# Stationary-weight products of a two-layer decoder: both parts of the activation in one 512-column pass, halves added by VectorE

## The chip, the cores and the metric

The kernel runs on one core of one Trainium2 chip. The metric is the device time of one execution in microseconds (us). The core has a matrix engine (TensorE, PE in the rows, with its weight loads as PEld), a vector engine (VectorE, DVE), a scalar engine (ScalarE, ACT), GpSimd (POOL) and a DMA queue driven by SyncE (SP). Matrix products are accumulated in PSUM banks of 128 x 512 fp32 values and taken out of them by ACT or DVE.

## The reference

Two decoder layers on x of 256 tokens by 1024 channels, in fp32. Each layer:

```python
proj = x @ w_in                       # q, k, v, u_ssm (512), u_pool (512), 3 x 1024 gate logits
attn_out = sliding_window_attention(q, k, v, sinks) @ w_br_attn
ssm_out  = glu_after_gelu(s5_ssm(u_ssm, ...), w_glu) @ w_br_ssm
pool_out = multiscale_pool(u_pool, pool_w, pool_scale) @ w_br_pool
gates = sigmoid(gate_logits + b_gate)            # one 1024-wide gate per branch
h = (gates[0]*attn_out + gates[1]*ssm_out + gates[2]*pool_out) @ w_o
x = layer_norm(alpha*x + h)
x = layer_norm(alpha*x + memory_cross_attention(x, mem, wq, wkv, wo))
f = swiglu(x, w_gu, w_down) if layer == 0 else moe_swiglu(x, ...)   # 2816 wide; top 2 of 8 experts
x = layer_norm(alpha*x + f)
```

## The kernel before

**Split products.** An fp32 product is made of fp32r products: each operand is split in a high part and the rest (`hi`, `lo`), and hi·hi, hi·lo and lo·hi are added up in PSUM. Weights come by DMA in 1 MB tiles (`raw`), and each half of a tile (1024 columns) is split when it is needed: ACT writes `whi` (`hi_of`, L218), then DVE writes `wlo` (`lo_of`, L221). `whi` and `wlo` have three buffers each, so the split of half n waits until PE has finished half n-3.

**Two kinds of product.** In the first kind (`mm3`, L280 to L283, called by `ws_gemm` at L398, by `ws_steps`, and by the FFN at L1148) a 128 x 128 piece of the weights is stationary and the 256 tokens of the activation move: three passes of 256 columns for each of 8 (or 4) steps over the contracted dimension (a k-step). The result, 128 output channels by 256 tokens, fills half of a PSUM bank and is then taken out by a function called sink. In the second kind (`xs_step`, `xs_end`, from L421) the activation is stationary and 512 columns of weights move.

**What the first kind computes**, outputs of 128 channels each: `us` (SSM input, 4 a layer, copied out of PSUM by ACT, L712), `up` (pool input, 4 a layer, ACT copy, L765), gates (24 a layer, ACT tanh from PSUM, L797), cross-attention keys and queries (`xkt`, `xqt`, 8 of each a layer, ACT copies, L1040 and L1054), and the FFN of layer 0 (22 blocks `hb`, each with a gate and an up half in the two halves of one bank: ACT silu, then a DVE multiply that reads the up half, L1154 and L1156). These have 8 k-steps each: 8 + 8 + 48 + 16 + 16 + 44 = 140 outputs, 1120 k-steps. The branch projections and the GLU have 4 k-steps.

**Order of the program.** 0 to 60 us: q/k/v, `us`, `up`. 60 to 225 us: the gates, the branch projections and attention, woven with the SSM. Then w_o, LayerNorm, cross-attention up to 375 us, the FFN from 375 to 575 us, and layer 1 from 590 us, with its MoE from some 945 us to the end. The order of each engine's instructions is fixed when the program is built, by a list scheduler that works on modelled durations; each engine then runs its list strictly in order.

**The SSM's parameters** are made by a generator (`ssm_params`): a chain of small DVE operations on `tmps`, then `spread` (L602 to L617), in which DVE makes products of 128 x 512 (`sp_p`: two multiplies and one add or subtract, L612 to L614) and ACT copies each into `bx` or `wx` (L617); PE transposes `bx` (L643, out of the block of ones `cst`) and ACT writes the transposes to `bt`. For layer 0 this runs at the start of the program; for layer 1 it is woven into the FFN, two steps of the generator for each `hb`.

Of the kernel before, what the change touches and what calls it, by code (L numbers as in the profile page):

```python
# [12 lines left out]
F32 = mybir.dt.float32  # L13
F32R = mybir.dt.float32r
# [6 lines left out]
P = 128  # L21
S = 256
# [174 lines left out]
def tile_trunk(ctx, tc, x_in, xt_in, memt_in, w_in, par_in, ln_in, lnt_in, wr_in, br_in, cst_in, out):  # L197
# [62 lines left out]
    def parts(raw):  # L260
# [16 lines left out]

        return get

    def mm3(ps, whi, wlo, xhi, xlo, first, last):  # L280
        T.matmul(ps, whi, xhi, start=first, stop=False)  # L281
        T.matmul(ps, whi, xlo, start=False, stop=False)  # L282
        return T.matmul(ps, wlo, xhi, start=False, stop=last)  # L283

    x = xp.tile([P, 2, D], F32, name="x")

    def split(raw, hi, lo):
        r3 = raw.rearrange("p (k t) -> p k t", k=KD)
        for k in range(0, KD, 2):
            hi_of(hi[:, k:k + 2, :], r3[:, k:k + 2, :])  # L290
            lo_of(lo[:, k:k + 2, :], r3[:, k:k + 2, :], hi[:, k:k + 2, :])


    xt = [xp.tile([P, KD, S], F32R, tag=n, name=n) for n in ("xhi", "xlo")]
    raws = [fifo.tile([P, CH], F32, tag="raw", name="raw") for _ in range(3)]
    for j, c, n in ((0, 0, 512), (1, 0, 1024), (0, 512, 512), (0, 1024, 512), (0, 1536, 512), (1, 1024, 1024),
                    (2, 0, 2048)):
# [12 lines left out]
    def layer_norm_in(l, i, f, end, kind, lp, r):  # L310
# [1 line left out]
        b = lp.tile([P, D], F32, name="lnb", bufs=1)  # L312
        nc.sync.dma_start(g, ln_in[l, 2 * i:2 * i + 1, :].to_broadcast([P, D]))
        nc.sync.dma_start(b, ln_in[l, 2 * i + 1:2 * i + 2, :].to_broadcast([P, D]))
        sh = [P, KD, S] if kind == "xt" else [P, 2, D]
        xhi = xp.tile(sh, F32R, tag="xhi", name="xhi")
        xlo = xp.tile(sh, F32R, tag="xlo", name="xlo")
        gt = lnt[:, l, 2 * i, :]
        bt = lnt[:, l, 2 * i + 1, :]
        H = [slice(n * 512, (n + 1) * 512) for n in range(2)]  # L320
# [77 lines left out]
    def ws_gemm(nob, kt, act, sink, first=0, w=None):  # L398
        per = 16 // kt
        for ob in range(first, nob):  # L400
            if ob % per == 0:
                w = wnext()
            ps = psw.tile([P, 512], F32, tag="wk", name="ps")
            for k in range(kt):
                c = ((ob % per) * kt + k) * P
                end = mm3(ps[:, :S], *w(c, c + P), act[0][:, k, :], act[1][:, k, :], k == 0, k == kt - 1)
            sink(ob, ps[:, :S])
        return w, end

    def ws_steps(nob, kt, act, sink):  # L410
# [260 lines left out]
    def mixer(l, xt, sc, sp, par, xk):  # L671
        with ExitStack() as es:
# [36 lines left out]
            us = wk.tile([P, 4, 4, SC], F32, tag="us", name="us", bufs=1)  # L709

            def us_sink(ob, ps):
                A.copy(us[:, :, ob, :], ps.rearrange("p (s k) -> p k s", k=4))  # L712

            ws_gemm(4, KD, xt, us_sink)
            ux = wk.tile([P, 4, 4, SC], F32, tag="ux", name="ux", bufs=1)
# [46 lines left out]
            GP.memset(sb[:, :, 0:16], 0.0)  # L762

            def up_sink(ob, ps):
                A.copy(up[:, ob, 16:], ps)  # L765

            ws_gemm(4, KD, xt, up_sink)
            V.tensor_add(sa[:, :, 16:], up[:, :, 16:], up[:, :, 15:S + 15])
# [23 lines left out]
            def gates(idx, gt=None):  # L792
                if gt is None:
                    gt = b8([P, 8, S], F32, "gate")

                def sink(ob, ps):
                    A.activation(gt[:, ob, :], ps, AF.Tanh, scale=0.5, bias=sp["bgh"][:, 8 * idx + ob:8 * idx + ob + 1])  # L797

                return gt, ws_steps(8, KD, xt, sink)

# [212 lines left out]
            wag.__exit__(None, None, None)  # L1013
            kvg = tc.tile_pool(name=f"kv{l}", bufs=1, reuse_waits="tile", side="right")
            kv = kvg.__enter__()
            mt = [kv.tile([P, KD, S], F32R, tag=n, name=n) for n in ("m_hi", "m_lo")]
            raw = fifo.tile([P, CH], F32, tag="raw", name="raw")
            nc.sync.dma_start(raw, memt_in)
            split(raw, *mt)
# [17 lines left out]
    def keys(mt, first, last, kt_=None, w=None):  # L1037
        if kt_ is None:
            kt_ = xp.tile([P, KD, S], F32, tag="k1", name="xkt")
        w, end = ws_gemm(last, KD, mt, lambda ob, ps: A.copy(kt_[:, ob, :], ps), first, w)  # L1040
        return kt_, w, end

    def cross(l, xt, kv, mt, kt_, w):
        with ExitStack() as es:
# [6 lines left out]

            keys(mt, 7 if l else 1, 8, kt_, w)
            qt = wk.tile([P, KD, S], F32, tag="xq", name="xqt", bufs=1)
            ws_gemm(8, KD, xt, lambda ob, ps: A.copy(qt[:, ob, :], ps))  # L1054

            wt = wk.tile([P, 2, 4 * S], F32, name="xwt", bufs=1)
            for m in range(2):
# [33 lines left out]
            if l == 0:  # L1091
                o_hi, o_lo = (wk.tile([P, KD, S], F32R, name=n, bufs=1) for n in ("o_hi", "o_lo"))
            else:
                o_hi, o_lo = (kv.tile([P, KD, S], F32R, tag=n, name=n) for n in ("m_hi", "m_lo"))
            for h in range(4):
                ps = psa.tile([P, 512], F32, tag="acc", name="ps")
                pv = ps.rearrange("p (c t) -> p c t", c=2)
# [17 lines left out]
    def ffn(l, xt, sc, mt, kt_):  # L1115
        with ExitStack() as es:
            mp = es.enter_context(tc.tile_pool(name="ff", bufs=2, reuse_waits="tile"))
            base = pos[0]
            accs = acc4()
            hs = {}  # L1120
            par = sc.tile([P, NPK], F32, name="par")
            nc.sync.dma_start(par, par_in[l + 1, :, 0:NPK])
            par2 = mp.tile([P, NPC - NPK], F32, tag="sp1", name="par2", bufs=4)
            nc.sync.dma_start(par2, par_in[l + 1, :, NPK:])
            tmps = mp.tile([P, 64, NT], F32, tag="sp1", name="tmps", bufs=4)
            sp = {}
            steps = ssm_params(sp, l + 1, sc, par, par2, tmps, *[lambda sh, *a, i=i: mp.tile(sh, F32, tag=f"sp{i}", name=a[-1], bufs=(1, 4, 4)[i])
                                         for i in range(3)])

            def down(i):  # L1130
                w = wnext(w_in[base + NFB + i])
                act = hs.pop(i)
                if i == NFB // 2 - 1:
                    return xs_end(accs, act, w, 0, 2, D, False)
                for kk in range(2):
                    xs_step(accs, act, w, kk * D, kk, D, i == 0 and kk == 0, False)

            for hb in range(NFB):
                w = wnext(w_in[base + hb])
                next(steps, None)  # L1140
                next(steps, None)
                ps = psw.tile([P, 512], F32, tag="wk", name="ps")
                for gu in range(2):
                    for k in range(KD):
                        c = (gu * KD + k) * P
                        mm3(ps[:, gu * S:(gu + 1) * S], *w(c, c + P), xt[0][:, k, :], xt[1][:, k, :],
                            k == 0, k == KD - 1)
                if hb % 2 == 0:  # L1148
                    hh = mp.tile([P, 2, S], F32R, tag="hh", name="hh", bufs=3)
                    hl = mp.tile([P, 2, S], F32R, tag="hl", name="hl", bufs=3)  # L1150
                    hs[hb // 2] = (hh, hl)
                hh, hl = hs[hb // 2]
                sl = mp.tile([P, S], F32, tag="sl", name="sl")
                A.activation(sl, ps[:, :S], AF.Silu)  # L1154
                h = mp.tile([P, S], F32, tag="h", name="h")
                V.tensor_mul(h, sl, ps[:, S:])  # L1156
                hi_of(hh[:, hb % 2, :], h)
                lo_of(hl[:, hb % 2, :], h, hh[:, hb % 2, :])
                if hb % 2 == 1 and hb >= 3:
                    down(hb // 2 - 1)  # L1160
            down(NFB // 2 - 1)
            for _ in steps:
# [308 lines left out]
```

## Time and profile before

| | |
|---|---|
| median of 3 runs | 1934.99 us (1934.83 to 1939.56) |
| the profiled execution | 1936.35 us, of which its span 1934.6 us |
| mean granted clock of TensorE | 0.987 |
| PE busy | 1877.8 us, 97% of the span |
| DVE busy | 1532.4 us, 79% |
| ACT busy | 1282.4 us, 66% |
| matmul instructions of the program | 10857 |

The span is the stretch that the profiler recorded; 1.75 us of the execution lie outside it. Busy time is summed over instructions, so it says how full an engine is, not who waits. A matmul's own duration overlaps that of the next one: the pace of PE is read from the distance between the starts of two matmuls.

### The profile page before, as it was taken

The numbers are of one execution on the slowest core, as the hardware profiler recorded it, in microseconds if no ns is written. First come the engines' busy times: TensorE is split into PE (matmuls) and PEld (weight loads), VectorE is DVE, ScalarE is ACT, GpSimd is POOL, SyncE is SP. The second block draws the span as 40 slices with busy tenths as digits, with TensorE's granted clock in tenths as the row PEclk, the third lists the DMA queues.
The fourth block names the chain that finished last, engine by engine and source line by source line (L and its number), as shares of the span: only waits on it lengthen the run. The fifth ranks groups of instructions, "written<-read, shape, count | busy, mean of one in ns | idle before, by whom it ended". The sixth has DMA issues, their size and how long they took to land.

```text
span 1934.6 us, 27897 instructions
## 1 busy us (share of the span) xinstructions
PE 1877.8 (97%) x10672; PEld 1630.0 (84%) x10672; DVE 1532.4 (79%) x1976; ACT 1282.4 (66%) x1673; POOL 110.9 (6%) x111
## 2 busy tenths in 40 slices
PE   7999999999999999998899999999999999999996
PEld 7998998899989988897688888888888888888875
DVE  7774774795557755765899999999999999999987
ACT  5666554556445555554687777777878778787774
POOL 4030000100004300001100000000000000000000
PEclk9999999999999999999999999999999999999998
DMA  7324554444555343594599998999989999899970
GB/s 256 132 90 147 189 211 149 181 175 153 186 185 183 115 161 113 196 408 158 211 375 369 358 376 319 373 375 353 375 321 374 375 356 374 319 375 364 387 271 24
DMA packets 74924, 503.37 MB, mean 260 GB/s; under 512 B 9504, under 2 KB 11808, under 8 KB 15264
## 3 DMA queue, kind: packets, MB, share of 16 engines
q1 hardware_dynamic: 74496, 500.43, 69.0%
q8 instruction: 85, 1.39, 0.3%
q0 software_dynamic: 144, 1.05, 0.2%
q14 instruction: 55, 0.45, 0.1%
q10 hardware_dynamic: 144, 0.05, 0.0%
HBM read 498.34 MB, written 1.05 MB: 258 GB/s over the span
## 4 chain that ended last, share of the span: by engine, by line
PE 89%; DVE 6%; ACT 3%; issue 2%; DMA 0%; POOL 0%; SPq 0%; ACTq 0%; POOLq 0%; DVEq 0%
PE ps L281 8%; PE ps L283 8%; PE ps L282 8%; PE pu L1302 5%; PE dn L450 5%; PE pu L1303 5%; PE pg L1303 5%; PE pu L1301 5%; PE pg L1302 5%; PE dn L451 5%; PE dn L452 5%; PE pg L1301 5%; DVE wlo L221 3%; PE acc L428 2%; PE acc L430 2%; PE acc L432 2%
## 5 line engine op out<-in xcount | busy, mean ns | idle before, releaser
L221 DVE TENSOR_TENSOR wlo<-raw,whi 128x1024 fp32r<-128x1024 f32 x926 | 1118.1, 1229 | 299.0 <-ACT whi L218 284.6
L218 ACT ACTIVATE whi<-raw 128x1024 fp32r<-128x1024 f32 x926 | 974.2, 1060 | 510.0 <-PE ps L282 183.9
L281 PE MATMUL ps<-xhi,whi 128*128 128x256 f32 x992 | 284.9, 289 | 9.0 <-ACT whi L218 8.6
L283 PE MATMUL ps<-xhi,wlo 128*128 128x256 f32 x992 | 284.4, 288 | 3.3 <-DVE wlo L221 3.3
L282 PE MATMUL ps<-xlo,whi 128*128 128x256 f32 x992 | 284.2, 287 | 0.0
L281 PEld LDWEIGHTS ps<-xhi,whi 128*128 128x128 f32 x992 | 192.5, 195 | 10.6 <-ACT whi L218 8.8
L283 PEld LDWEIGHTS ps<-xhi,wlo 128*128 128x128 f32 x992 | 192.7, 195 | 4.6 <-DVE wlo L221 3.8
L282 PEld LDWEIGHTS ps<-xlo,whi 128*128 128x128 f32 x992 | 193.0, 195 | 0.8 <-issue 0.3
L1302 PE MATMUL pu<-wlo,xg 128*128 128x512 f32 x448 | 175.8, 392 | 2.7 <-DVE wlo L221 2.7
L451 PE MATMUL dn<-wlo,hth 128*128 128x512 f32 x448 | 177.9, 400 | 0.1
L1302 PE MATMUL pg<-wlo,xg 128*128 128x512 f32 x448 | 176.3, 394 | 1.4 <-DVE wlo L221 1.4
L1303 PE MATMUL pg<-whi,xg 128*128 128x512 f32 x448 | 175.6, 392 | 0.6 <-DVE xg L1254 0.6
L1301 PE MATMUL pg<-whi,xg 128*128 128x512 f32 x448 | 175.0, 391 | 0.0
L1301 PE MATMUL pu<-whi,xg 128*128 128x512 f32 x448 | 174.7, 390 | 0.0
L1303 PE MATMUL pu<-whi,xg 128*128 128x512 f32 x448 | 174.6, 390 | 0.0
L452 PE MATMUL dn<-whi,htl 128*128 128x512 f32 x448 | 173.8, 391 | 0.0
L450 PE MATMUL dn<-whi,hth 128*128 128x512 f32 x448 | 139.3, 390 | 0.0
L1302 PEld LDWEIGHTS pu<-wlo,xg 128*128 128x128 f32 x448 | 84.0, 188 | 27.6 <-DVE wlo L221 6.6
L1302 PEld LDWEIGHTS pg<-wlo,xg 128*128 128x128 f32 x448 | 84.1, 188 | 24.1 <-DVE wlo L221 3.8
L1301 PEld LDWEIGHTS pu<-whi,xg 128*128 128x128 f32 x448 | 84.1, 188 | 17.8
L450 PEld LDWEIGHTS dn<-whi,hth 128*128 128x128 f32 x448 | 83.9, 188 | 17.9
L1301 PEld LDWEIGHTS pg<-whi,xg 128*128 128x128 f32 x448 | 84.2, 188 | 17.3
(520 smaller groups left out, 2874.9 us busy)
## 6 DMA issues: line engine op xcount, KB each, us to landing
raw<-in_w SPq DMA_DIRECT2D x462, 1024.0 KB, 4.9
lng<-in_ln SPq DMA_DIRECT2D x6, 512.0 KB, 6.5
lnb<-in_ln SPq DMA_DIRECT2D x6, 512.0 KB, 7.3
raw<-in_memt SPq DMA_DIRECT2D x2, 1024.0 KB, 5.1
raw<-in_xt SPq DMA_DIRECT2D x4, 256.0 KB, 5.9
raw<-in_w SPq DMA_DIRECT2D x2, 512.0 KB, 6.3
ux<-us SPq DMA_DIRECT2D x32, 32.0 KB, 2.1
yg<-ux SPq DMA_DIRECT2D x32, 32.0 KB, 1.9
```

What stands on the lines that cost most here:

```text
L218: return A.activation(dst, src, AF.Copy, scale=scale)
L221: return V.tensor_sub(dst, src, hi.bitcast(F32))
L281: T.matmul(ps, whi, xhi, start=first, stop=False)
L282: T.matmul(ps, whi, xlo, start=False, stop=False)
L283: return T.matmul(ps, wlo, xhi, start=False, stop=last)
L428: T.matmul(accs[m][n], ah, wh, start=first, stop=False)
L450: T.matmul(ps, ah, wh, start=first, stop=False)
L451: T.matmul(ps, ah, wl, start=False, stop=False)
L452: return T.matmul(ps, al, wh, start=False, stop=last)
L1301: T.matmul(ps, xg[0][:, k, :], wh, start=(k == 0), stop=False)
L1302: T.matmul(ps, xg[0][:, k, :], wl, start=False, stop=False)
L1303: T.matmul(ps, xg[1][:, k, :], wh, start=False, stop=(k == KD - 1))
```

## The change

The two parts of an activation become one tile with two halves (`pair`: `xhl` for x, `mhl` for the memory). For products with 8 k-steps `mm2` takes the place of `mm3`: one pass of 512 columns multiplies `whi` with both parts and writes both halves of a PSUM bank, and one pass of 256 columns adds `wlo`·`xhi` into the second half. When the output is taken out, DVE adds the halves (`total`, a `tensor_reduce` over an axis of two). This replaces the 48 ACT copies of `us`, `up`, `xkt` and `xqt`, comes ahead of the 48 gate tanh, which then work in place in SBUF, and comes twice in each FFN block, ahead of silu and of the multiply. An FFN block now takes two PSUM banks instead of one. Products with 4 k-steps stay as they were. The program has 9737 matmuls after the change.

```diff
+    def pair(pool, shape, tag):
+        t = pool.tile([P, 2] + shape, F32R, tag=tag, name=tag)
+        return t[:, 0], t[:, 1], t
+    def mm2(ps, whi, wlo, both, first, last):
+        T.matmul(ps, whi, both, start=first, stop=False)
+        return T.matmul(ps[:, 1], wlo, both[:, 0], start=False, stop=last)
+
+    def total(dst, ps):
+        return V.tensor_reduce(dst, ps.rearrange("p c t -> p t c"), axis=AX.X, op=ALU.add)
...
-            ps = psw.tile([P, 512], F32, tag="wk", name="ps")
+            ps = psw.tile([P, 2, S], F32, tag="wk", name="ps")
...
-                end = mm3(ps[:, :S], *w(c, c + P), act[0][:, k, :], act[1][:, k, :], k == 0, k == kt - 1)
-            sink(ob, ps[:, :S])
+                if kt == KD:
+                    end = mm2(ps, *w(c, c + P), act[2][:, :, k], k == 0, k == kt - 1)
+                else:
+                    end = mm3(ps[:, 0], *w(c, c + P), act[0][:, k], act[1][:, k], k == 0, k == kt - 1)
+            sink(ob, ps if kt == KD else ps[:, 0])
...
-                A.copy(us[:, :, ob, :], ps.rearrange("p (s k) -> p k s", k=4))
+                V.tensor_reduce(us[:, :, ob, :], ps.rearrange("p c (s k) -> p k s c", k=4), axis=AX.X, op=ALU.add)
...
-                A.copy(up[:, ob, 16:], ps)
+                total(up[:, ob, 16:], ps)
...
-                    A.activation(gt[:, ob, :], ps, AF.Tanh, scale=0.5, bias=sp["bgh"][:, 8 * idx + ob:8 * idx + ob + 1])
+                    total(gt[:, ob, :], ps)
+                    A.activation(gt[:, ob, :], gt[:, ob, :], AF.Tanh, scale=0.5,
+                                 bias=sp["bgh"][:, 8 * idx + ob:8 * idx + ob + 1])
...
-                ps = psw.tile([P, 512], F32, tag="wk", name="ps")
-                for gu in range(2):
+                pgu = [psw.tile([P, 2, S], F32, tag="wk", name="ps") for _ in range(2)]
+                for gu, ps in enumerate(pgu):
                     for k in range(KD):
                         c = (gu * KD + k) * P
-                        mm3(ps[:, gu * S:(gu + 1) * S], *w(c, c + P), xt[0][:, k, :], xt[1][:, k, :],
-                            k == 0, k == KD - 1)
+                        mm2(ps, *w(c, c + P), xt[2][:, :, k], k == 0, k == KD - 1)
...
-                A.activation(sl, ps[:, :S], AF.Silu)
+                total(sl, pgu[0])
+                A.activation(sl, sl, AF.Silu)
                 h = mp.tile([P, S], F32, tag="h", name="h")
-                V.tensor_mul(h, sl, ps[:, S:])
+                total(h, pgu[1])
+                V.tensor_mul(h, sl, h)
```

The change also moves instructions, since the scheduler orders them anew. One place is in the FFN of layer 0, where the SSM parameters of layer 1 are made. On DVE before, the last of the small operations (`tmps`) are followed by the `sp_p` products, between the weight halves `wlo_4549` and `wlo_4585`:

```order
L571 TENSOR_TENSOR tmps_4020<-tmps_4020 128x48
L570 TENSOR_TENSOR tmps_4020<-tmps_4020 128x48
L572 TENSOR_TENSOR tmps_4020<-tmps_4020 128x48
L612 TENSOR_TENSOR sp_p_4505<-par2_4018,tmps_4020 128x512
L221 TENSOR_TENSOR wlo_4549<-raw_4490,whi_4548 128x1024
L613 TENSOR_TENSOR sp_p_4506<-par2_4018,tmps_4020 128x512
L612 TENSOR_TENSOR sp_p_4512<-par2_4018,tmps_4020 128x512
L613 TENSOR_TENSOR sp_p_4513<-par2_4018,tmps_4020 128x512
L614 TENSOR_TENSOR sp_p_4505<-sp_p_4505,sp_p_4506 128x512
```

On DVE after, the same operations (now at L584 to L587 and L627 to L629) stand behind `wlo_4257`, six weight halves further on, and all 24 `sp_p` products follow there in a row; the first add (`sp_p_4044` from itself and `sp_p_4045`) is the fifth of them, the second behind these rows:

```order
L221 TENSOR_TENSOR wlo_4257<-raw_4220,whi_4256 128x1024
L579 TENSOR_TENSOR tmps_3624<-tmps_3624 128x16
L587 TENSOR_TENSOR tmps_3624<-tmps_3624 128x32
L584 TENSOR_TENSOR tmps_3624<-tmps_3624 128x48
L586 TENSOR_TENSOR tmps_3624<-tmps_3624 128x48
L582 TENSOR_TENSOR tmps_3624<-tmps_3624 128x48
L583 TENSOR_TENSOR tmps_3624<-tmps_3624 128x48
L585 TENSOR_TENSOR tmps_3624<-tmps_3624 128x48
L587 TENSOR_TENSOR tmps_3624<-tmps_3624 128x48
L627 TENSOR_TENSOR sp_p_4044<-par2_3622,tmps_3624 128x512
L628 TENSOR_TENSOR sp_p_4045<-par2_3622,tmps_3624 128x512
L627 TENSOR_TENSOR sp_p_4051<-par2_3622,tmps_3624 128x512
```

On ACT before, `bx` is written between the weight halves `whi_4600` and `whi_4643`:

```order
L218 ACTIVATE whi_4584<-raw_4582 128x1024
L1154 ACTIVATE sl_4484<-ps_4425 128x256
L218 ACTIVATE whi_4600<-raw_4582 128x1024
L617 ACTIVATE bx_4503<-sp_p_4505 64x32x16 x2
L218 ACTIVATE hh_4482<-h_4486 128x256
L617 ACTIVATE bx_4503<-sp_p_4512 64x32x16 x2
L218 ACTIVATE whi_4643<-raw_4616 128x1024
```

On ACT after, it is written directly behind `whi_4256`, the high part that `wlo_4257` is made from:

```order
L218 ACTIVATE whi_4170<-raw_4142 128x1024
L218 ACTIVATE hh_4019<-h_4103 128x256
L218 ACTIVATE whi_4190<-raw_4142 128x1024
L218 ACTIVATE whi_4256<-raw_4220 128x1024
L632 ACTIVATE bx_4042<-sp_p_4044 64x32x16 x2
L632 ACTIVATE bx_4042<-sp_p_4051 64x32x16 x2
L659 COPY bt0_4039<-ps_4144 128x512
```

On PE before, the transposes that read `bx` (L643) come inside the products with the half `whi_4600`, two halves behind `whi_4548`, whose split stands among the first `sp_p`:

```order
L432 MATMUL acc_4015<-whi_4584,hl_4277 128x512
L428 MATMUL acc_4012<-whi_4600,hh_4276 128x512
L428 MATMUL acc_4013<-whi_4600,hh_4276 128x512
L428 MATMUL acc_4014<-whi_4600,hh_4276 128x512
L428 MATMUL acc_4015<-whi_4600,hh_4276 128x512
L643 MATMUL ps_4618<-cst_70,bx_4503 128x128 x4
L643 MATMUL ps_4624<-cst_70,bx_4503 128x128 x4
L238 MATMUL pg_4502<-cx_4492,bx_4503 128x32
```

On PE after, they (now L658) come directly behind the last product with `whi_4126`. This is the half whose buffer `whi_4256` takes (4126, 4170, 4190, 4256 follow one another), and the products with 4170 and 4190 come behind the transposes:

```order
L445 MATMUL acc_3618<-wlo_4127,hh_3839 128x512
L445 MATMUL acc_3619<-wlo_4127,hh_3839 128x512
L447 MATMUL acc_3618<-whi_4126,hl_3840 128x512
L447 MATMUL acc_3619<-whi_4126,hl_3840 128x512
L658 MATMUL ps_4144<-cst_70,bx_4042 128x128 x4
L658 MATMUL ps_4150<-cst_70,bx_4042 128x128 x4
L238 MATMUL pg_4041<-cx_4031,bx_4042 128x32
L658 MATMUL ps_4156<-cst_70,bx_4042 128x128 x4
```

So the place of the transposes among PE's products stayed nearly the same, while what they wait for moved from well ahead of them on DVE and ACT to behind a weight split that itself waits for the product just ahead of them.

## Rows read from the trace of the kernel before

**Rows 1.** The page: busy time of each engine, share of the span, instructions.
```profile
PE 1877.8 (97%) x10672; PEld 1630.0 (84%) x10672; DVE 1532.4 (79%) x1976; ACT 1282.4 (66%) x1673; POOL 110.9 (6%) x111
```
**Rows 2.** Busy time by stretch: PE, PEld, DVE, ACT, POOL, granted clock, DMA share, GB/s.
```profile
0.00:945.00 945.00, 908.11 (x6283) 838.54 (x6284) 625.53 (x1101) 518.21 (x852) 108.92 (x109) 0.98 0.49 176
...
375.00:575.00 200.00, 199.21 (x1421) 186.87 (x1420) 128.29 (x246) 103.82 (x148) 8.03 (x4) 1.00 0.50 178
50.00:225.00 175.00, 172.39 (x1353) 165.13 (x1352) 119.66 (x197) 112.07 (x205) 20.14 (x22) 0.97 0.36 124
```
**Rows 3.** Timeline of PE, first kind: start, duration, line, out<-in.
```profile
600.71 0.28 PE L281 MATMUL ps<-xhi,whi 128*128 128x256 f32 x1
...
601.07 0.28 PE L281 MATMUL ps<-xhi,whi 128*128 128x256 f32 x1
```
**Rows 4.** Timeline of PE, passes with a moving operand in pieces (`y_hi`).
```profile
717.32 0.28 PE L281 MATMUL ps<-y_hi,whi 128*128 128x256 f32 x1
...
717.68 0.28 PE L281 MATMUL ps<-y_hi,whi 128*128 128x256 f32 x1
```
**Rows 5.** Timeline of PE, passes of 512 columns (q/k/v).
```profile
24.81 0.39 PE L428 MATMUL acc<-whi,xhi 128*128 128x512 f32 x1
...
25.49 0.39 PE L428 MATMUL acc<-whi,xhi 128*128 128x512 f32 x1
```
**Rows 6.** The same in the FFN.
```profile
416.42 1.09 PE L428 MATMUL acc<-whi,hh 128*128 128x512 f32 x4
417.35 0.63 PE L430 MATMUL acc<-wlo,hh 128*128 128x512 f32 x2
```
**Rows 7.** Reduces of 512 values from PSUM, and an ACT copy: shortest/median/longest ns.
```profile
L900 DVE TENSOR_REDUCE mx<-ps x12: 691/692/693, 147.2 to 769.1; 128x2 f32<-128x512 f32 x8, 128x4 f32<-128x512 f32 x4
L712 ACT COPY us<-ps x8: 354/357/373, 15.5 to 603.6; 128x256 f32<-128x256 f32 x8
```
**Rows 8.** Timeline of DVE in the FFN: the SSM parameters of layer 1.
```profile
408.29 0.20 DVE L572 TENSOR_TENSOR tmps<-tmps 128x48 f32<-128x48 f32 x1
408.41 0.68 DVE L612 TENSOR_TENSOR sp_p<-par,tmps 128x512 f32<-128x512 f32 x1
409.01 1.23 DVE L221 TENSOR_TENSOR wlo<-raw,whi 128x1024 fp32r<-128x1024 f32 x1
410.16 0.68 DVE L613 TENSOR_TENSOR sp_p<-par,tmps 128x512 f32<-128x512 f32 x1
410.76 0.68 DVE L612 TENSOR_TENSOR sp_p<-par,tmps 128x512 f32<-128x512 f32 x1
```
**Rows 9.** Timeline of ACT there; in brackets the idle time before, and its releaser.
```profile
407.92 1.06 ACT L218 ACTIVATE whi<-raw 128x1024 fp32r<-128x1024 f32 x1 [1.70 <-PE ps L282]
...
414.58 1.26 ACT L617 ACTIVATE bx<-sp_p 64x512 f32<-64x512 f32 x2
```
**Rows 10.** Timeline of PE there: the transposes of `bx`.
```profile
420.15 1.03 PE L643 MATMUL ps<-cst,bx 128*128 128x128 f32 x8
```
**Rows 11.** Timeline of PE: two longer waits.
```profile
595.00 0.39 PE L283 MATMUL ps<-xhi,wlo 128*128 128x256 f32 x1 [2.34 <-DVE wlo L221]
...
722.46 0.58 PE L281 MATMUL ps<-y_hi,whi 128*128 128x256 f32 x1 [2.85 <-ACT glt L998]
```
**Rows 12.** Busy time and granted clock (third from the end) behind these waits.
```profile
595.40:598.90 3.50, 3.50 (x19) 3.50 (x19) 3.50 (x3) 0.00 (x0) 3.50 (x4) 0.51 0.00 0
721.70:728.60 6.90, 6.14 (x29) 6.14 (x30) 2.85 (x6) 3.89 (x11) 0.00 (x0) 0.51 0.08 12
```
**Rows 13.** Timeline of PE at 76 us: waits for the SSM parameters of layer 0.
```profile
76.92 0.43 PE L844 MATMUL ps<-ux,bt 128*128 128x64 f32 x2 [0.87 <-ACT bt L644]
78.09 1.09 PE L643 MATMUL ps<-cst,x 128*128 128x128 f32 x8 [0.74 <-ACT x L617]
```
**Rows 14.** Busy time by stretch in the first 40 us of the FFN (columns of rows 2).
```profile
375.00:395.00 20.00, 19.21 (x161) 19.01 (x160) 18.52 (x53) 11.74 (x18) 6.22 (x3) 1.00 0.51 182
...
405.00:415.00 10.00, 10.00 (x86) 10.00 (x85) 9.73 (x30) 4.83 (x6) 0.00 (x0) 1.00 0.63 211
```

More of the change, by code (lines that the diff above doesn't have):

```diff
@@ L283, in mm3, with split @@
         return T.matmul(ps, wlo, xhi, start=False, stop=last)
+    def mm2(ps, whi, wlo, both, first, last):
[3 more added lines that the diff above has]
+        return V.tensor_reduce(dst, ps.rearrange("p c t -> p t c"), axis=AX.X, op=ALU.add)
     x = xp.tile([P, 2, D], F32, name="x")
-    def split(raw, hi, lo):
+    def split(raw, hi, lo, _):
         r3 = raw.rearrange("p (k t) -> p k t", k=KD)
@@ L291, in split @@
             lo_of(lo[:, k:k + 2, :], r3[:, k:k + 2, :], hi[:, k:k + 2, :])
-    xt = [xp.tile([P, KD, S], F32R, tag=n, name=n) for n in ("xhi", "xlo")]
+    xt = pair(xp, [KD, S], "xhl")
     raws = [fifo.tile([P, CH], F32, tag="raw", name="raw") for _ in range(3)]
@@ L314, in layer_norm_in @@
         nc.sync.dma_start(b, ln_in[l, 2 * i + 1:2 * i + 2, :].to_broadcast([P, D]))
-        sh = [P, KD, S] if kind == "xt" else [P, 2, D]
-        xhi = xp.tile(sh, F32R, tag="xhi", name="xhi")
-        xlo = xp.tile(sh, F32R, tag="xlo", name="xlo")
+        xhi, xlo, both = pair(xp, [KD, S] if kind == "xt" else [2, D], "xhl")
         gt = lnt[:, l, 2 * i, :]
@@ L384, in layer_norm_in @@
             return xhi, xlo, pl, dv
-        return xhi, xlo
+        return xhi, xlo, both
     lnt = cp.tile([P, L, 6, KD], F32, name="lnt")
@@ L1015, in mixer @@
             kv = kvg.__enter__()
-            mt = [kv.tile([P, KD, S], F32R, tag=n, name=n) for n in ("m_hi", "m_lo")]
+            mt = pair(kv, [KD, S], "mhl")
             raw = fifo.tile([P, CH], F32, tag="raw", name="raw")
@@ L1039, in keys @@
             kt_ = xp.tile([P, KD, S], F32, tag="k1", name="xkt")
-        w, end = ws_gemm(last, KD, mt, lambda ob, ps: A.copy(kt_[:, ob, :], ps), first, w)
+        w, end = ws_gemm(last, KD, mt, lambda ob, ps: total(kt_[:, ob, :], ps), first, w)
         return kt_, w, end
@@ L1053, in cross @@
             qt = wk.tile([P, KD, S], F32, tag="xq", name="xqt", bufs=1)
-            ws_gemm(8, KD, xt, lambda ob, ps: A.copy(qt[:, ob, :], ps))
+            ws_gemm(8, KD, xt, lambda ob, ps: total(qt[:, ob, :], ps))
             wt = wk.tile([P, 2, 4 * S], F32, name="xwt", bufs=1)
@@ L1093, in cross @@
             else:
-                o_hi, o_lo = (kv.tile([P, KD, S], F32R, tag=n, name=n) for n in ("m_hi", "m_lo"))
+                o_hi, o_lo, _ = pair(kv, [KD, S], "mhl")
             for h in range(4):
```

## The prediction, made before the changed kernel ran

> **What bounds the kernel now.** I read the page's first part, then busy time by stretch, then PE's timelines, because the change touches only products that end before the MoE. Up to 945 us PE is busy for 908 us at a mean granted clock of 0.98, DVE for 626 us, ACT for 518 us [rows 2]; over the whole span PE is busy 97% and DVE 79% [rows 1]. So up to 945 us the number of passes on PE sets the time, and its gaps come second: 37 us in all. The stretches differ. In the FFN PE is busy for 199.2 of 200 us [rows 2], though DVE is as good as full in its first 40 us: 18.52 of 20, then 9.73 of 10 [rows 14]. There DVE makes the SSM parameters of layer 1, and PE doesn't notice: the first `sp_p` starts at 408.41 and the transposes that need it at 420.15 [rows 8, 10], so this chain has some 12 us from its first product to its reader and DVE is busy with it in the spare time of the weight splits. The change saves PE passes everywhere and loads DVE in just this place. The MoE works by 512-column passes already and is not touched; I take it to shift as a whole.
>
> **PE's passes: -14.6 us.** Three passes of 256 columns take 601.07 - 600.71 = 0.36 us [rows 3], 120 ns each. Three of 512 columns take 25.49 - 24.81 = 0.68 us [rows 5], 227 ns each. At 2.4 GHz the columns themselves are 106.7 and 213.3 ns, so either pass carries some 13 ns on top. A k-step goes from 360 to 227 + 120 = 347 ns and saves one such 13 ns: over 1120 k-steps 14.6 us. Of the products in question 352 k-steps lie in the FFN, where four passes of 512 columns take 417.35 - 416.42 = 0.93 us, 232 ns each [rows 6]; if the new passes run like these there, 5 ns come back 352 times, 1.9 us, and if they do everywhere, the saving is 1120 x 8 ns = 9.0 us. At 234 ns, a little beyond these rows, it would be 6.7 us. I take 227: like the passes of rows 5 the new ones read x, whereas rows 6 are passes with the FFN's own activations. The moving operand now consists of two pieces that lie apart; `y_hi` also moves in pieces, and three of its passes take 717.68 - 717.32 = 0.36 us as well [rows 4], so I add nothing for that.
>
> The Trainium skill (TensorE: Matmul & The Clock Gate, section "Wait — 56ns, not 53.3ns?") speaks against the gain: warm matmuls start N / 2.4 GHz plus about 2.5 ns apart. By that a k-step saves 2.5 ns and the whole change 2.8 us (an estimate from that page). The rows show 13 ns on top at either width, so here they decide.
>
> **DVE's totals, beside PE: +84 to 97 us of work.** The nearest row is the reduce of 512 values out of PSUM at 692 ns [rows 7]; neighbouring DVE operations start earlier than their predecessor's recorded end: 512-column products of 0.68 us start 0.60 us apart [rows 8]. 140 totals cost 84 us by the one, 97 us by the other. The new reduce reads its pairs 256 columns apart, which no row shows; twice the price, 1.2 us each, is the upper end that I carry. In return ACT loses 48 copies of 0.36 us [rows 7], 17 us. DVE goes from 626 to some 715 us of 945: not the bound on average, since a product of 8 k-steps gives 8 x 347 = 2.78 us of PE and asks 1.15 (a split, 410.16 - 409.01 [rows 8]) + 0.60 us of DVE. So nearly all of it is hidden; where it isn't is the next point.
>
> The Trainium skill (VectorE: DVE Perf Modes, section "Rules for kernel authors") says of a `tensor_reduce` on the hot path to expect the slowest kind of DVE operation and to consider restructuring. If that meant the upper end here, the totals would be 168 us, and the rival with DVE below would get nearer.
>
> **FFN, SSM parameters: +7.8 us.** This is where the full DVE [rows 14] gets two totals more in each block, 1.2 us of 8.3 us. The order shows the result: the chain slid behind `wlo_4257`, while PE's transposes stayed behind the products with `whi_4126`. Since `whi_4256` needs the buffer of `whi_4126`, everything from there on is in series with PE standing still. From the end of PE's last product with `whi_4126`: the high part on ACT 1.06 us [rows 9]; the low part on DVE 1.15 us; eight small operations at 0.12 us (408.41 - 408.29 [rows 8]), 0.96 us; four `sp_p` at 0.60 and the add that ends the first at 0.68 us, 3.08 us; two copies into `bx` 1.26 us [rows 9]. That is 7.5 us; for handoffs and because DVE gets there late (17 small operations stand ahead of `wlo_4257` as well) I add 0.3. Before, the same chain was 12 us ahead, so its price was nothing. The bounds: 0, if DVE and ACT were ready far earlier, which the buffer excludes unless PE itself waits before; 10 us, if those 17 operations count in full. Next in line, `wlo_4277` stands behind all 24 `sp_p` (14.4 us) and a total. That ends some 19.6 us after the same moment, and PE, which after its wait has the transposes and three halves of products of 2.8 us, needs it at about that time; I put nothing for it.
>
> **The clock behind that wait: +2.6 us.** After a wait of 2.34 us PE ran at 0.51 of its full clock, that is 1.2 GHz, for 3.5 us; after one of 2.85 us for 6.9 us [rows 11, 12]. Half of such a stretch is lost: 1.75 to 3.45 us. I take the middle; the bounds are 0 and 3.45.
>
> **Layer 0's start at 75 us: +2.1 us.** The transposes of layer 0 wait 0.87 and 0.74 us already [rows 13]. There a total for every gate now stands on DVE between the `sp_p` products, and the second add that `bx` waits for stands behind the total of the gate that PE does just before. Waits of some 2 us become some 4. The bounds are 0 and 4 more.
>
> **The rest: +1.1 us.** Sinks that were one ACT instruction become DVE, then ACT, so keys, queries and gates are ready up to 0.7 us later; PE notices where a consumer follows at once. Between 50 and 225 us DVE has 119.7 us of 175 [rows 2] and gets 24 totals more, 14 to 17 us, so the SSM's quads of operations may push a weight split late once or twice. Bounds 0 and 5; near the lower end, because the three buffers of the weight halves hold some 8 us of PE's work.
>
> **Sum.** -14.6 + 7.8 + 2.6 + 2.1 + 1.1 = -1.0 us. Against the profiled execution of 1936.35 us (span 1934.6) that gives 1935.35; the median is 1934.99 us, 1.4 lower, so I forecast 1934.0 us. A measurement of this kernel can tell about 0.3% (5.8 us) from no change: this lies within.
>
> **Rivals.**
> *The FFN wait isn't there*, or is short, since PE reaches that place later than I think relative to DVE. For it: PE is fed by three buffers and waits little before. Against: the order, which leaves no way around `whi_4256`. Then 7.8 + 2.6 go: -11.4 us, 1923.6 us; with a wait of 2 us and no slow clock, 1925.6.
> *DVE becomes the bound* where its work comes in bunches (the start of layer 0, the SSM quads of both layers, the FFN's first 40 us): each total stands in line with the splits, so a split comes late, and PE not only waits but runs at 1.2 GHz behind it. It decides from a wait of about 2.3 us on, the shorter of rows 11. Three such places at 2.3 + 2.6 us, less the 3.2 us that the sum already holds: +11.5 us, 1945.5 us. For it: 9.73 of 10 us [rows 14], and the reduce at 1.2 us would add 1.2 us more to each FFN block, which lengthens the slide. Against: the average of 76%.
> *The 512-column pass costs 234 ns*: saving 6.7 instead of 14.6, +6.9 us, 1941.9 us. For it rows 6, against rows 5.
> *A pass costs only 2.5 ns on top of its columns*: saving 2.8 us, +10.8 us, 1945.8 us. Against it rows 3 and 5 alike. The Trainium skill's rule above is this one.
>
> **How the numbers follow.** The forecast 0.40; no FFN wait 0.30; DVE in bunches 0.21; the dearer pass 0.07; the 2.5 ns rule 0.02. The forecast's own range, with the bounds of its terms, is 1928 to 1942; I share it as 0.02 faster, 0.35 within 0.3% and 0.03 slower. The first rival is faster by over 0.3% (0.30), the second slower with 0.20 of its 0.21; the third gives 0.02 within 0.3% and 0.05 slower, the fourth 0.02 slower. Together: faster 0.32, within 0.3% 0.38, slower 0.30. The range from 1923 to 1946 leaves out the far ends of the two larger rivals, about 0.2.
>
> **What will show it.** Passes: 512-column passes of `xhl` starting 227 ns apart, k-steps 347 ns apart. Totals: `tensor_reduce` of about 0.69 us, 140 of them. FFN: a gap of 7 to 8 us on PE ahead of L658 near 410 us, released by ACT's `bx`, and a stretch of clock 0.5 behind it. Layer 0: waits ahead of L658 at some 74 us that add up to 4 us. MoE as long as before. I would be wrong first in the FFN wait: in the order it is certain, but its length rests on when DVE gets there; and after that in how many splits come late because of a total ahead of them.

## The result, and the profile after

The changed kernel takes 1955.26 us (median of 5 runs, 1953.6 to 1957.03) against 1935.79 us for the kernel before in the same comparison: 1.0101 times as long, 95% interval 1.0088 to 1.0113. It is slower by 19.5 us and outside the range given (1923 to 1946); the forecast was 1 us faster, too little to be told from no change.

First the page of the changed kernel: its span, then busy time of each engine as in [rows 1].

```profile
span 1954.7 us, 25768 instructions
...
PE 1880.5 (96%) x9552; PEld 1575.7 (81%) x9552; DVE 1617.6 (83%) x2116; ACT 1277.1 (65%) x1625; POOL 110.4 (6%) x111
```

PE has 1120 passes fewer in the records and is yet busy 2.7 us longer than in [rows 1], and it is idle 1954.7 - 1880.5 = 74.2 us, where it was 56.8. So two things were lost: 17.4 us of standing still, and a clock that made the fewer passes last longer. The mean granted clock fell from 0.987 to 0.979. The rows show the clock at full or at half, so what the mean lacks, times the span, is the time lost to half clock: 0.013 x 1934.6 = 25 us before, 0.021 x 1954.7 = 41 us after, 16 us more (some 4 of them in time in which PE stood still anyway).

Up to the MoE, busy time by stretch of the changed kernel (columns as in [rows 2]): the whole first part; 20 us around the second LayerNorm; then three stretches at half clock, behind that LayerNorm, in the FFN and behind the third LayerNorm.

```profile
0.00:964.60 964.60, 910.36 (x5163) 784.25 (x5164) 710.88 (x1241) 513.02 (x804) 108.44 (x109) 0.96 0.47 172
365.30:385.30 20.00, 16.64 (x84) 13.66 (x83) 17.73 (x29) 11.07 (x17) 1.10 (x2) 0.83 0.28 106
369.00:375.80 6.80, 5.31 (x20) 4.36 (x19) 5.91 (x11) 3.52 (x7) 0.55 (x1) 0.50 0.40 142
...
430.50:444.20 13.70, 9.26 (x41) 8.90 (x42) 12.31 (x21) 7.37 (x12) 0.00 (x0) 0.50 0.05 20
...
597.70:604.50 6.80, 5.13 (x18) 4.55 (x19) 5.63 (x8) 3.45 (x6) 0.65 (x2) 0.50 0.59 205
```

The first row beside that of [rows 2]: all 19.6 us are lost ahead of the MoE, and DVE's 711 us are what the prediction had worked out (715). The MoE shifts as a whole.

**The passes** save a little less than they were to. Timeline of PE in the changed kernel, in layer 1's queries and in the FFN:

```profile
850.01 0.39 PE L293 MATMUL ps<-xhl,whi 128*128 128x512 f32 x1
850.24 0.27 PE L294 MATMUL ps<-xhl,wlo 128*128 128x256 f32 x1
...
851.05 0.40 PE L293 MATMUL ps<-xhl,whi 128*128 128x512 f32 x1
```

```profile
500.69 0.40 PE L293 MATMUL ps<-xhl,whi 128*128 128x512 f32 x1
500.92 0.28 PE L294 MATMUL ps<-xhl,wlo 128*128 128x256 f32 x1
...
501.75 0.39 PE L293 MATMUL ps<-xhl,whi 128*128 128x512 f32 x1
```

Three k-steps take 1.04 us in the one, 347 ns each, and 1.06 us in the other, 353 ns; before it was 360 [rows 3]. These are samples. Taken from the starts of the matmuls in the whole trace, single k-steps at full clock last from about 340 to 362 ns in both places, with a mean of 351 in layer 1's queries and 352 in the FFN; over all of them the mean is 351, and 359.6 before.

**The FFN wait** stands where the order put it. Timelines of the changed kernel, PE first, then ACT, then DVE:

```profile
426.61 0.62 PE L447 MATMUL acc<-whi,hl 128*128 128x512 f32 x2
434.94 1.94 PE L658 MATMUL ps<-cst,bx 128*128 128x128 f32 x8 [7.72 <-issue]
```

```profile
427.31 1.06 ACT L218 ACTIVATE whi<-raw 128x1024 fp32r<-128x1024 f32 x1 [1.72 <-PE acc L447]
433.58 2.56 ACT L632 ACTIVATE bx<-sp_p 64x512 f32<-64x512 f32 x4 [5.21 <-DVE sp_p L629]
```

```profile
428.40 1.22 DVE L221 TENSOR_TENSOR wlo<-raw,whi 128x1024 fp32r<-128x1024 f32 x1
...
430.45 0.69 DVE L627 TENSOR_TENSOR sp_p<-par,tmps 128x512 f32<-128x512 f32 x1
...
432.86 1.28 DVE L629 TENSOR_TENSOR sp_p<-sp_p 128x512 f32<-128x512 f32 x2
```

PE's last product ends at 427.2; ACT makes the high part at once (427.31), DVE the low part, the small operations and the `sp_p`; ACT writes `bx` at 433.58, and PE goes on at 434.94 after 7.72 us. The row names no releaser ("issue"); that it is `bx` follows from the order and from the first two copies, which take 1.26 us [rows 9] and so end at some 434.84. Where PE went on at 420.15 before [rows 10], nothing of this chain was in its way.

**What the prediction had no place for** is at the LayerNorms. DVE in the changed kernel, second and third LayerNorm of layer 0:

```profile
361.46 0.69 DVE L238 BATCH_NORM_STATS2 bst<-lny 128x6 f32<-128x512 f32 x1
365.61 0.69 DVE L297 TENSOR_REDUCE xkt<-ps 128x256 f32<-128x512 f32 x1 [3.46 <-PE ps L294]
366.22 0.20 DVE L238 BATCH_NORM_AGGREGATE bmv<-bst 128x2 f32<-128x12 f32 x1
```

```profile
593.36 0.69 DVE L297 TENSOR_REDUCE xkt<-ps 128x256 f32<-128x512 f32 x1 [3.40 <-PE ps L294]
593.97 0.20 DVE L238 BATCH_NORM_AGGREGATE bmv<-bst 128x2 f32<-128x12 f32 x1
```

and before, at the third:

```profile
573.90 0.69 DVE L238 BATCH_NORM_STATS2 bst<-lny 128x6 f32<-128x512 f32 x1
574.63 0.21 DVE L238 BATCH_NORM_AGGREGATE bmv<-bst 128x2 f32<-128x12 f32 x1
```

While DVE works out a LayerNorm, PE is kept busy by one product of the cross-attention keys, which needs nothing of the LayerNorm: the cover. Its output was copied by ACT. Now it is a total on DVE, and the scheduler put that total ahead of the LayerNorm's aggregation. DVE, with the statistics done, stands still for 3.4 us until the cover has ended on PE, and only then goes on with the LayerNorm for which PE will wait in turn. The cover has become what the LayerNorm waits for. Waits of PE around the third LayerNorm (565 to 590 us before, 580 to 610 us after; in us, times, longest), before and after:

```profile
PE pt L238 <- ACT lny L238: 1.8, 1, 1.8
```

```profile
PE pt L238 <- ACT lny L238: 4.5, 2, 2.6
```

**A smaller one** is at the start of layer 1, where the total of `us` stands behind two long LayerNorm operations on DVE (L390, 613.44) and PE waits for its PSUM bank, 3.62 us against 2.34 for another reason there before [rows 11]. DVE and PE of the changed kernel:

```profile
613.44 3.31 DVE L390 TENSOR_TENSOR x<-x,lnb 128x1024 f32<-128x1024 f32 x2
616.67 1.27 DVE L727 TENSOR_REDUCE us<-ps 128x256 f32<-128x512 f32 x2
```

```profile
617.49 1.26 PE L293 MATMUL ps<-xhl,whi 128*128 128x512 f32 x2 [3.62 <-DVE us L727]
```

**At layer 0's start** the waits of [rows 13] grew from 0.87 and 0.74 us to 1.06 and 2.09:

```profile
77.08 0.43 PE L861 MATMUL ps<-ux,bt 128*128 128x64 f32 x2 [1.06 <-ACT bt L659]
79.60 1.97 PE L658 MATMUL ps<-cst,x 128*128 128x128 f32 x8 [2.09 <-ACT x L632]
```

### The profile page after: what moved, and what is told of

The parts are those of the page before. It is cut to its first block, busy times and chain, and to the rows that moved or that the text cites. A ratio compares the mean times of both kernels' runs of the same rounds, so it can differ in the third digit from the quotient of the medians.

```text
span 1954.7 us, 25768 instructions
## 1 busy us (share of the span) xinstructions
PE 1880.5 (96%) x9552; PEld 1575.7 (81%) x9552; DVE 1617.6 (83%) x2116; ACT 1277.1 (65%) x1625; POOL 110.4 (6%) x111
## 3 DMA queue, kind: packets, MB, share of 16 engines
q8 instruction: 77, 1.26, 0.3%
## 4 chain that ended last, share of the span: by engine, by line
PE 71%; DVE 6%; issue 2%; ACT 1%; POOL 0%; POOLq 0%; DVEq 0%; ACTq 0%
PE ps L293 8%; PE pu L1320 5%; PE dn L465 5%; PE pu L1321 5%; PE pu L1319 5%; PE pg L1321 5%; PE pg L1320 5%; PE dn L466 5%; PE dn L467 5%; PE pg L1319 5%; PE ps L294 4%; DVE wlo L221 2%; PE acc L445 2%; PE acc L443 2%; PE acc L447 2%
## 5 line engine op out<-in xcount | busy, mean ns | idle before, releaser
L293 PE MATMUL ps<-xhl,whi 128*128 128x512 f32 x992 | 364.0, 408 | 13.0 <-ACT whi L218 7.3
L294 PE MATMUL ps<-xhl,wlo 128*128 128x256 f32 x992 | 283.7, 287 | 2.1 <-DVE wlo L221 1.9
L293 PEld LDWEIGHTS ps<-xhl,whi 128*128 128x128 f32 x992 | 191.2, 193 | 59.0 <-ACT whi L218 8.5
L294 PEld LDWEIGHTS ps<-xhl,wlo 128*128 128x128 f32 x992 | 192.2, 194 | 5.3 <-DVE wlo L221 3.5
L1319 PEld LDWEIGHTS pg<-whi,xg 128*128 128x128 f32 x448 | 84.1, 188 | 17.3
L1321 PEld LDWEIGHTS pg<-whi,xg 128*128 128x128 f32 x448 | 84.1, 188 | 17.0 <-DVE xg L1272 1.5
L466 PEld LDWEIGHTS dn<-wlo,hth 128*128 128x128 f32 x448 | 84.2, 188 | 16.7 <-DVE wlo L221 0.6
```

The lines of the kernel that those rows point to most:

```text
L293: T.matmul(ps, whi, both, start=first, stop=False)
L294: return T.matmul(ps[:, 1], wlo, both[:, 0], start=False, stop=last)
L466: T.matmul(ps, ah, wl, start=False, stop=False)
L1319: T.matmul(ps, xg[0][:, k, :], wh, start=(k == 0), stop=False)
L1321: T.matmul(ps, xg[1][:, k, :], wh, start=False, stop=(k == KD - 1))
```

## Experiments

The kernel before was run again beside each of these, with medians from 1935.2 to 1936.5 us. By the intervals, a difference between two of the runs is known to some 3 us.

Theory A: the passes gain what the rows of PE show, and DVE's totals lose more than that. Its rival, theory B: the wide passes themselves lose it. Later, theory C: it isn't the totals' work, but the place in DVE's order of a few of them and of what they displaced.

### Passes without totals

```diff
-                total(sl, pgu[0])
-                A.activation(sl, sl, AF.Silu)
+                A.activation(sl, pgu[0][:, 1], AF.Silu)
...
-                total(h, pgu[1])
-                V.tensor_mul(h, sl, h)
+                V.tensor_mul(h, sl, pgu[1][:, 1])
```

(and likewise for `us`, `up`, the gates, `xkt` and `xqt`; one half of each output is left out, so the result is not the product)

> The passes of the change alone: products with 8 k-steps run as one pass of 512 and one of 256 columns, but the halves are not added; each output is read from the second half by the instruction that read it before (ACT copy, tanh, silu, DVE multiply), so the whi x xhi part is left out of the result. Theory A (the passes save some 8.5 ns a k-step, and DVE's totals bring the waits and the slow clock): faster than before by 9.5 us, about 1926 us (1922 to 1930), gaps on PE and half-clock stretches up to 960 us as before, 29 and 16 us. Theory B (the wide passes themselves bring waits, by two PSUM banks a block or by needing both parts of x at once): the FFN wait of 7.7 us or the new waits around the LayerNorms stay, 1940 us or more.

Measured: 1927.88 us against 1936.16 us before, ratio 0.9958 (0.9946 to 0.997): 8.1 us faster. PE and DVE on its page:

```profile
PE 1871.6 (97%) x9552; PEld 1568.9 (81%) x9552; DVE 1531.8 (79%) x1976; ACT 1285.0 (67%) x1675; POOL 112.1 (6%) x111
```

Between 370 and 575 us its trace shows no wait of PE at all, and DVE is as busy as in [rows 1]. The passes gain 8.1 / 1120 = 7.2 ns a k-step (5.8 to 10.5 us by the interval); theory B falls.

### Totals without the wide passes

```diff
-        T.matmul(ps, whi, both, start=first, stop=False)
+        if first:
+            T.matmul(ps, whi, both, start=True, stop=False)
+        else:
+            T.matmul(ps[:, 0], whi, both[:, 0], start=False, stop=False)
+            T.matmul(ps[:, 1], whi, both[:, 1], start=False, stop=False)
         return T.matmul(ps[:, 1], wlo, both[:, 0], start=False, stop=last)
```

> The totals of the change alone: the halves of a PSUM bank are filled by three passes of 256 columns as before (only the first of 8 k-steps uses the 512-column pass, which starts the bank), and DVE adds them. Theory A: all the waits of the change and none of the saving but for 140 k-steps, so the changed kernel's time plus 980 x 8.5 ns = 8.3 us, about 1963 us (1957 to 1968). Theory B: no new waits, 1935 us (1932 to 1940).

Measured: 1964.59 us, ratio 1.0144 (1.0118 to 1.017). As theory A had it: with the passes nearly as before, the totals cost 28 us, and PE's waits are those of the changed kernel (7.7 us in the FFN, 8.3 at the LayerNorms between 225 and 640 us, 3.2 for `us`). The two runs together account for the result: -8 for the passes, +28 for the totals.

### The FFN as before, and the FFN alone

The changed kernel with the FFN as before (silu and the multiply read PSUM again):

```diff
-                pgu = [psw.tile([P, 2, S], F32, tag="wk", name="ps") for _ in range(2)]
-                for gu, ps in enumerate(pgu):
+                ps = psw.tile([P, 512], F32, tag="wk", name="ps")
+                for gu in range(2):
...
-                        mm2(ps, *w(c, c + P), xt[2][:, :, k], k == 0, k == KD - 1)
+                        mm3(ps[:, gu * S:(gu + 1) * S], *w(c, c + P), xt[0][:, k, :], xt[1][:, k, :],
+                            k == 0, k == KD - 1)
```

> The change everywhere but in the FFN, which runs as before (three passes of 256 columns, silu and multiply from PSUM). Theory A, with the FFN wait as its largest part: the wait of 7.7 us and the 4.6 us lost to the slow clock behind it go, 352 x 8.5 ns = 3.0 us come back, 1955.3 - 12.3 + 3.0 = 1946 us (1942 to 1950), and the waits at the LayerNorms, at the start of layer 1 and near 130 us stay. Rival (those other waits follow from the FFN's delayed work): they go too, 1932 us or less.

Measured: 1947.14 us, ratio 1.0048 (1.0033 to 1.0063). No wait of PE is left between 385 and 575 us. The other waits stayed (8.9 us at the LayerNorms, 3.6 for `us`), so they don't follow from the FFN.

The kernel before with the FFN alone changed (`if kt == KD` for `mm2` switched off, sinks as before):

> The change in the FFN alone. In its order the first products for bx stand one weight half earlier than in the changed kernel, with splits between them. Theory A: a wait of 4 to 8 us in the FFN with a slow stretch behind it (2 to 5 us lost), saving 3.0 us: before plus 3 to 10 us, 1938 to 1946 us. Rival (the FFN's totals are hidden unless DVE is loaded elsewhere as well): faster than before by about 3 us, 1932 us.

Measured: 1944.08 us, ratio 1.0037 (1.0022 to 1.0053), with a wait of 6.3 us ahead of the transposes. By the medians the FFN alone loses 8 us and the rest 11, together 19 of the 19.5 of the change; by the ratios it is 7 and 9, each with some 3 us either way.

### The FFN wait taken away

The generator of the SSM parameters is advanced by one step a block, so the transposes come later in PE's order:

```diff
             for hb in range(NFB):
                 w = wnext(w_in[base + hb])
                 next(steps, None)
-                next(steps, None)
```

> The changed kernel, but in the FFN the SSM parameters of layer 1 are advanced by one step of their generator for each block instead of two. In the order the transposes that read bx then come some twelve weight halves behind the first products for bx instead of ahead of them. Theory A (the FFN wait is that chain in series): the wait of 7.7 us and the 4.6 us lost to the slow clock behind it go, nothing else does: 1955.3 - 12.3 = 1943 us (1939 to 1947). Rival (DVE is simply too full in the FFN, the wait turns up elsewhere in it): 1950 us or more.

Measured: 1941.6 us, ratio 1.0034 (1.0022 to 1.0046), 13.7 us less than the changed kernel, and within the 12.3 us expected by what its runs differ. DVE still does all 44 totals of the FFN; PE waits in the FFN no more. What PE waits for between 378 and 590 us is at the LayerNorm:

```profile
PE pt L238 <- ACT lny L238: 3.9, 2, 2.6
```

The control, the same edit to the kernel before:

> Control: the kernel before, with the SSM parameters of layer 1 advanced by one step a block. It had no wait in the FFN, so nothing should change: 1936 us (1933 to 1939). If it gains, a gain of the run above is not due to the new form.

Measured: 1935.49 us, ratio 0.9999 (0.9986 to 1.0013). The edit is worth nothing without the change.

### The keys as before

With `wide=False`, `ws_gemm` makes the product by `mm3`:

```diff
-        w, end = ws_gemm(last, KD, mt, lambda ob, ps: total(kt_[:, ob, :], ps), first, w)
+        w, end = ws_gemm(last, KD, mt, lambda ob, ps: A.copy(kt_[:, ob, :], ps), first, w, wide=False)
```

> The changed kernel, but the cross-attention keys (xkt) are computed as before, with three passes of 256 columns and an ACT copy. Theory C (the totals of the keys that cover the LayerNorms stand on DVE ahead of the LayerNorm's own statistics, so these wait until the cover is over): the PE waits at the second and third LayerNorm of layer 0 return to what they were before, gaps of 2.5 us and 2.7 us and 3.6 us of slow clock go, 128 x 8.5 ns = 1.1 us come back, and the FFN wait shrinks by about 1 us as in the run with the change in the FFN alone: 1955.3 - 8.8 + 1.1 - 1 = 1946.6 us (1943 to 1950). Rival (the totals add to DVE's load in general): the 16 key totals are 16 of 140, so at most 2 to 3 us, 1952 us or more.

Measured: 1944.29 us, ratio 1.0038 (1.0023 to 1.0053): 11 us less than the changed kernel for 16 of 140 totals. Not all of it is the LayerNorms: the FFN wait is 6.2 us in its trace instead of 7.7. Waits for `lny` between 225 and 385 us, changed kernel first, then this one, where the second LayerNorm's wait is as short as before:

```profile
PE pt L238 <- ACT lny L238: 3.9, 3, 1.4
```

```profile
PE pt L238 <- ACT lny L238: 0.4, 2, 0.2
```

### The same totals in another place

All 140 totals are kept; those of the four covers are ordered behind the LayerNorm's last statistic (`guard[0]`, to which the weight splits are tied as well):

```diff
+    later = []
+
+    def pay():
+        while later:
+            Line(guard[0])(total, *later.pop(0))
...
-        kt_, w, end = keys(mt, 0, 1)
+        kt_, w, end = keys(mt, 0, 1, put=lambda *a: later.append(a))
         xt = layer_norm(l, 1, lambda m, n: accs[m][n], end)
+        pay()
```

(and likewise at the other three)

> The changed kernel with every total kept, but the totals of the four key products that cover a LayerNorm are ordered on DVE behind the LayerNorm's own statistics. DVE has the same work, only its order differs. Theory C (place, not load): the waits at the LayerNorms of layer 0 go (gaps at 366 to 372 us back to 1 us, at 594 to 599 us back to 1.8 us, without the slow stretch at 369 us), about -7 us: 1948 us (1945 to 1951). Rival (the load of the totals): as the changed kernel, 1955 us.

Measured: 1944.17 us, ratio 1.0048 (1.0032 to 1.0065), 11 us less than the changed kernel, where 7 were expected; 4 of the 140 totals moved, none removed. DVE at the second LayerNorm:

```profile
357.81 0.69 DVE L238 BATCH_NORM_STATS2 bst<-lny 128x6 f32<-128x512 f32 x1
358.54 0.21 DVE L238 BATCH_NORM_AGGREGATE bmv<-bst 128x2 f32<-128x12 f32 x1
...
362.95 0.16 DVE L238 SCALAR_TENSOR_TENSOR bnb<-bmv,brs 128x1 f32<-128x1 f32 x1 [0.75 <-POOL brs L238]
363.03 0.68 DVE L297 TENSOR_REDUCE xkt<-ps 128x256 f32<-128x512 f32 x1
```

The aggregation follows its statistic at once, and the idle 3.46 us ahead of the total are gone, since the total comes when the product has ended. PE's waits between 225 and 390 us fall from 4.5 to 1.9 us. This is theory C: the same work on DVE, another place (the scheduler orders what stands around it anew).

The 4 us beyond the 7 expected need not belong to the LayerNorms. The FFN wait is still there, but the stretch at half clock that goes with it is shorter in this profiled execution, 6.8 us instead of 13.7:

```profile
427.22 1.94 PE L658 MATMUL ps<-cst,bx 128*128 128x128 f32 x8 [7.72 <-issue]
```

```profile
424.30:431.10 6.80, 3.88 (x20) 3.91 (x20) 6.77 (x12) 4.27 (x7) 0.00 (x0) 0.50 0.01 2
```

Both remedies together:

> As the run before, and the SSM parameters of layer 1 advanced by one step a block: all 1120 k-steps in the new form, all 140 totals on DVE. If the FFN chain and the LayerNorms' cover hold most of the loss: 1941.6 - 7 = 1934.5 us (1931 to 1937), what is left over the run of the passes alone (1927.9) being the wait for us at the start of layer 1 and the start of layer 0. Rival (140 totals are simply too much for DVE): 1940 us or more.

Measured: 1934.25 us against 1935.21 us before, ratio 0.9994 (0.9984 to 1.0004). With the 140 totals on DVE (1615.4 us busy on its page, 1532.4 before) the loss of the change is gone. Of the 28 us that the totals cost, the place of the FFN's chain and of four totals held 21. Without the FFN wait the four totals are worth 7.4 us (1941.6 to 1934.25), as theory C had expected, and not 11.

With `us` and `up` as before besides:

> As the run before, but us and up as in the kernel before (three passes, ACT copies): 1056 k-steps in the new form, 1056 x 7.5 ns = 7.9 us saved. If the totals of us cost the 3.6 us wait at the start of layer 1 (2.3 before) and the wait at 37 us: 1930 us (1927 to 1933), the fastest of all. Rival (us and up don't matter): 1934 us.

Measured: 1935.78 us, ratio 1.0003 (0.9993 to 1.0013). This expectation was wrong: taking the totals of `us` and `up` away gains nothing, though the wait of 3.5 us for `us` goes out of the trace. In its place PE waits 2.3 us for `wlo`, as before the change, and its waits at layer 0's start grow from 3.2 to 4.9 us.

### Versions that beat both kernels

Gates, queries and FFN in the new form, `us`, `up` and keys as before, one generator step a block:

> The new form in the gates, the queries and the FFN (108 of 140 outputs, 864 of 1120 k-steps); us, up and the keys as before; the SSM parameters advanced by one step a block. Theory A with C: no FFN wait, no wait at the LayerNorms, none behind us: passes save 864 x 8.5 ns = 7.3 us, the start of the gates keeps some 2 to 6 us of gaps and slow clock: 1936.2 - 7.3 + 4 = 1933 us (1929 to 1937). Rival (gate and FFN totals alone load DVE enough): 1940 us or more.

Measured: 1931.02 us against 1936.53 us, ratio 0.998 (0.9968 to 0.9992). And with `us` and `up` in the new form as well:

> Everything in the new form but the keys (992 of 1120 k-steps, 124 of 140 totals), and the SSM parameters advanced by one step a block. The fastest run so far (gates, queries and FFN) also kept us and up as before. If us and up don't matter, their 64 k-steps a layer save another 0.9 us: 1930 us (1928 to 1933). If the totals of us cost a wait at the start of layer 1 (3.6 against 2.3 us) and behind it: 1933 us or more.

Measured: 1932.37 us against 1935.69 us, ratio 0.9974 (0.9962 to 0.9987). Both are faster than the kernel before, by 4 to 5 us, and cannot be told apart; that `us` and `up` don't matter agrees with the run above.

## Why the prediction was wrong

Run by run, the loss of 19.5 us is made up of: -8.1 for the passes (1927.9 us), +6.4 that stay with both remedies (1934.3), +7.4 for the place of four totals at the LayerNorms (1941.6), +13.7 for the FFN wait with its clock (1955.3). The prediction had -14.6 for the passes, 7.8 + 2.6 for the FFN, 2.1 for layer 0's start and 1.1 for all the rest.

**The passes** were rightly read in kind and too large in size: -8.1 us by the run of the passes alone instead of -14.6. The term took 347 ns for every k-step. The mean in the trace is 351 ns, in the FFN as elsewhere, as the 232 ns of [rows 6] had said, and the bound worked out from those rows for everywhere, -9.0, is near what came; -14.6 lies outside the measured interval. The prediction gave [rows 5] the preference because the new passes read x; all of the new passes outside the keys do, and they are not faster for it. What remains between some 9 us of pace and 8.1 of time, the runs cannot resolve. (Its 1.9 us for 5 ns in 352 k-steps should be 1.8; nothing rests on it.)

**The FFN wait** was predicted as 7.8 us and is 7.72, link for link. Here the order gave what waits for what, and rows of the old trace gave the durations.

**The clock behind it** was put at 2.6 us by two stretches that followed waits of 2.3 and 2.9 us [rows 11, 12]. With this wait 13.7 us ran at 0.50, of which PE was busy 9.26: 4.6 us lost. The step was to take the middle of two stretches of shorter waits. That a longer wait has a longer stretch does not follow either: with four totals moved the same wait of 7.72 us had 6.8 us, of which PE was busy 3.88, so 1.9 lost. What sets the length stays open.

**The total's price** was right: 0.69 us in the trace, no dearer for halves that lie 256 columns apart, and DVE's load came to the 711 us that were foreseen.

**Layer 0's start** was put at +2.1 us; its two waits grew by 1.5 us, from 1.6 to 3.2.

**"The rest: +1.1 us" is the step that failed**; it had no price for slow clock either. Next to it stands the pass term, 6.5 us too large. The step said that PE notices a late sink "where a consumer follows at once", looked at the three buffers of the weights, and took a value near its lower end. It asked how full DVE is and who reads the total. It didn't ask what stands *behind* each total on DVE while the total waits for PE. At the LayerNorms that is the LayerNorm itself. The key's total is read by nobody for a long time, and still held up everything, because it waits in line. The runs show its price: 7.4 us when four totals move and the FFN wait is gone, 11 us when it is there. In the old trace the place could have been found: ACT copied `xkt` in the midst of the third LayerNorm, and the question what else its new engine has to do just then would have led to it.

**Of the rivals**, DVE in bunches had the right sign, and its sentence "each total stands in line with the splits" is half of the mechanism. Its places (SSM quads, the FFN's first 40 us) and its reason, a load near 100%, were not it: DVE stood still at the place. Its 1945.5 us came short by 10 us: it kept the passes' 14.6 us and left out the LayerNorms. (Its +11.5 us is counted from the forecast, the sums of the other rivals from the kernel before.) The rival of passes at 234 ns, a saving of 6.7 us, lies within the measured interval of 5.8 to 10.5, as the bound of 9.0 does; alone it gave 1941.9. The rival of 2.5 ns a pass, a saving of 2.8 us, lies outside it.

**Open** are some 6 us: the run with both remedies takes 1934.3 us, the passes alone 1927.9. Leaving the keys out gets some 2 to 4 of them back (1931 to 1932 us), `us` and `up` nothing; at the gates' start PE still waits some 3 to 5 us, and at 39 us there is a wait of 2.25 us for `wlo` that the run of the passes alone does not have. Which of the remaining totals hold the rest was not tried.

## What to carry to other kernels

An instruction that is moved to another engine takes a place in that engine's line, and from then on everything behind it waits for what it waits for: look at what stands behind it, not only at who reads its result. Work that covers another stage must not be taken out by the engine that the covered stage runs on, unless it is ordered behind that stage. And since a saving of 7 ns a step, 8 us in all, was spent by a single wait of 7.7 us with its slow clock, the order after the change is worth reading wherever a short serial stage meets the engine that got more work.

## What the runs showed of the hardware

One 512-column pass and one 256-column pass together take from about 340 to 362 ns with the same instructions, within one stretch of the program; the mean is 351 ns, against 359.6 ns for three passes of 256 columns before. What sets the spread was not tried.

Stretches at half clock are not tied to the order of the program alone. The same wait of 7.72 us went with 13.7 us of half clock in one kernel and 6.8 us in another. And in the profiled execution of the changed kernel the stretch from 133.5 us ran at 0.50 without a PE wait over 0.6 us in the 10 us ahead of it; in that of the run with four totals moved, whose order first differs at the LayerNorm at some 258 us, the same stretch ran at full clock. Busy time by stretch, changed kernel first, then that run:

```profile
133.50:140.30 6.80, 6.80 (x27) 6.22 (x27) 6.73 (x11) 3.29 (x6) 3.15 (x4) 0.50 0.26 105
```

```profile
133.50:140.30 6.80, 6.50 (x43) 5.65 (x43) 6.70 (x12) 4.92 (x7) 1.78 (x3) 1.00 0.03 12
```

So one profiled execution can lose some 3 us to slow clock that another doesn't, and small differences between kernels were read from the medians, not from profiles.
